# Expert stage of a one-layer diffusion transformer: its pools in another place, each tile waiting for the bytes it takes over

## The chip, the cores and the metric

The kernel runs on one core of a Trainium2 chip. The metric is the device time of one execution in microseconds (us). A core has five engines with instruction streams of their own: TensorE (PE, matmuls), VectorE (DVE), ScalarE (ACT), GpSimd (POOL) and SyncE (SP, which here only issues transfers). Sixteen DMA engines move data between HBM and the on-chip memory SBUF; matmuls write to the accumulator memory PSUM. Each engine runs its instructions in order, and an instruction that waits holds up everything behind it on that engine.

## The reference

It is one layer on 1024 tokens of width 1024, with a context of 256 tokens: modulation from a condition, windowed attention with a short convolution beside it, a merge, and then a layer of product-key experts, with a norm at the end. The part that matters here is the last one:

```python
def chunk(t):                                    # t: 128 tokens of h
    T = t.shape[0]
    qh = (t @ w_q).reshape(T, 8, 2, 128)         # 8 heads, two halves of a query
    s = jnp.einsum('thpd,hpnd->thpn', qh, sub_keys)
    s_top, i_top = lax.top_k(s, 16)              # 16 of 128 keys for each half
    cand = s_top[:, :, 0, :, None] + s_top[:, :, 1, None, :]
    cand_idx = i_top[:, :, 0, :, None] * 128 + i_top[:, :, 1, None, :]
    best, pos = lax.top_k(cand.reshape(T, 8, 256), 16)
    idx = jnp.take_along_axis(cand_idx.reshape(T, 8, 256), pos, axis=-1)
    g = jax.nn.softmax(best, axis=-1)
    ue, ve = u_tab[idx], v_tab[idx]              # 16384 experts, rows of 1024
    act = jax.nn.gelu(jnp.einsum('thkd,td->thk', ue, t), approximate=False)
    return jnp.einsum('thk,thkd->td', g * act, ve)
```

## The kernel before

**Two halves.** The tokens are worked on in two halves of 512. For each half the kernel computes queries and scores (`bank` in PSUM, split by ACT into a 16-bit high part `qqh` and by DVE into a low part `qql`), and finds the top 16 keys on DVE (`sl`, `sv`, `si`). The scores use weights `whl` that SP loads one after another (line 170) into four buffers of the pool `wts`. For half 0 the gates are then scattered into a dense table in HBM, `gd` (written by POOL from `ge`, line 1008), while the scores of half 1 are still being worked out.

**The expert stage** begins at 1096 us of the trace and runs to the end. It treats most experts densely: 128 slots of 128 experts. For a slot SP loads 128 rows of `v` (line 1131), two slots ahead the rows of `u` (`u_t`, line 1114), for every 16 slots two gate tiles `gt` (line 1091), and PE makes `ups` = u times the tokens. ACT applies GELU (`gel`), DVE multiplies `gel` by `gt`, ACT writes the 16-bit high part `wdh` and DVE the low part `wdl`; `v` is split in the same way into `vh` (ACT) and `vl` (DVE); and PE sums the products of these parts into PSUM tiles `res` and `vps`. The slots run first with all 512 tokens of half 0, then with 384 of half 1.

**Slots 0 to 2** have their GELU values prepared earlier (`UPRE` = 3): they lie in HBM as `ged` and only have to be loaded (line 1168). The `u` rows of slots 3 to 5 are split into `whl` buffers before the stage (`u_first`, line 1453): their 72 matmuls, `ups<-h,whl`, are the first PE work of the stage.

**Beside the slots** run the gates of half 1: DVE finds the best candidates (`cand`, `best`, `pos`), turns them into indices (`eq`, `fi`, `fig`, `ci`), and POOL gathers 512 tiles of `u` rows and 128 of `v` rows by these indices (`row`, line 916), which DVE multiplies with the tokens (`row<-row,hn`) and adds up.

**Pools.** SBUF is cut into pools that open and close as a stack, from a left and a right end. Before the expert stage the left end holds, counted in KB of each partition behind the constants, `wts` (24 KB, with the `whl` buffers), `half1` (32 KB), and on the bytes of `half0` the pool `gate0`, in which the gates of half 0 are worked on. All of them are closed before the stage, and `psF` and others in PSUM too. The stage opens `acc` (14 KB: sums `part` and buffers `wdh`) and on top of it `dense0`, with everything else: loads, `gel`, `gt`, splits. So the first tiles of `dense0` lie on bytes of `wts`. By default the first use of any tile in a new pool waits until everything that used the released pools below it has ended. `gate1` is opened on the right for the gates of half 1.

**Order.** The framework's scheduler decides the order of the instructions of each engine up to slot 8 of the stage (`PIN_FROM`); from there on the code pins it. Nearly all instructions of PE, DVE and ACT are recorded by a helper (class `Meter`), so they all have line 72; they are told apart by their tiles.

Of the kernel before, what the change touches and what calls it, by code (L numbers as in the profile page):

```python
# [11 lines left out]
F16 = mybir.dt.float16  # L12
# [6 lines left out]
PSUM = bass.MemoryType.PSUM  # L19

D = 1024
# [10 lines left out]
NDENSE = 512  # L32
NMIX = 384
# [9 lines left out]
SUB = 4  # L43
# [71 lines left out]
def drain(gen):  # L115
    while True:
        try:
            next(gen)
        except StopIteration as e:
            return e.value  # L120


class K:
# [9 lines left out]
        self.waiting = []  # L133
        self.turned = None

    def pool(self, name, side=None, space=None, bufs=1):
        kw = {}
        if side is not None:
            kw["side"] = side
        if space is not None:  # L140
            kw["space"] = space
        g = self.tc.tile_pool(name=name, bufs=bufs, **kw)
        p = g.__enter__()
        return g, p
# [870 lines left out]
    def open_gate(self, name, side, ge_bufs):  # L1015
        nc, a = self.nc, self.a
        self.ge_bufs = ge_bufs
        g, self.pg = self.pool(name, side=side)
        p = self.pg
        io32 = p.tile([128, 128], F32, name="io32", tag="dot", bufs=1)  # L1020
        nc.sync.dma_start(io32, a["iota"])
        io16 = p.tile([128, 128], F16, name="iotas")
        nc.vector.tensor_copy(io16, io32)
        self.iota = io16.rearrange("p (a b) -> p a b", b=REP).unsqueeze(1).to_broadcast([128, TB, 128 // REP, REP])
        self.cand = p.tile([128, 8, NCAND], F32, name="cand", tag="cand", bufs=1)
        nc.vector.memset(self.cand[:, :, 16:128], NEG)
        self.iota16 = p.tile([128, 16, 16], F16, name="iota16")
        nc.vector.tensor_copy(self.iota16, io32[:, 0:16].unsqueeze(2).to_broadcast([128, 16, 16]))
        return g
# [104 lines left out]
    def split_v(self, i1, v32, p):  # L1134
        if v32 is None:
            return self.vparts[i1]
        vh = p.tile([128, D], F16, name="vh", tag="vh", bufs=2 * SUB)
        vl = p.tile([128, D], F16, name="vl", tag="vl", bufs=2 * SUB)
        self.nc.scalar.activation(vh, v32, AF.Copy, scale=16.0)
        self.late[0].append((vl, v32, 16.0, vh))  # L1140
        if i1 >= 128 - 2 * SUB:
            self.vparts[i1] = vh, vl
        return vh, vl
# [13 lines left out]
    def slot_dense(self, i1, p, pv, outs):  # L1157
        nc = self.nc
        nb = NDENSE // 32
        hh, hl = self.h2h[0], self.h2l[0]  # L1160
        self.load_u(i1 + 2, p)
        v32 = self.load_v(0, i1, p)
        self.block_gates(0, i1, p)
        wh = self.pac.tile([128, NDENSE], F16, name="wdh", tag="wdh", bufs=2 * SUB)
        wl = p.tile([128, NDENSE], F16, name="wdl", tag="wdl", bufs=2 * SUB)
        ge = p.tile([128, NDENSE], F32, name="gel", tag="gel", bufs=2)
        if i1 < UPRE:
            nc.sync.dma_start(ge, self.ged[i1])
        else:
            uh, ul = self.uparts.pop(i1)  # L1170
            ps = pv.tile([128, 512], F32, name="ups", tag="v", bufs=3)
            for k in range(8):
                self.mm3(ps, uh[:, k, :], ul[:, k, :], hh[:, k, :], hl[:, k, :], k == 0, k == 7)
        self.lows(1)
        self.lows(0)
        if outs:
            yield 0
        if i1 >= UPRE:
            nc.scalar.activation(ge, ps, AF.Gelu, scale=2.0 ** -12)
        self.split_u(i1 + 2, p)  # L1180
        vh, vl = self.split_v(i1, v32, p)
        ends = []
        for k, out in enumerate(outs):
            ends.append(out())
            if k == 0:
                yield 0
        for end in ends:
            end()
        gev = ge.rearrange("p (b t) -> p b t", t=16)
        for q in range(2):  # L1190
            qs = slice(nb * q, nb * q + nb)
            nc.vector.tensor_mul(gev[:, qs, :], gev[:, qs, :], self.gts[q][:, :, i1 % GR, :])
        nc.scalar.activation(wh, ge, AF.Copy, scale=256.0)
        self.late[0].insert(0, (wl, ge, 256.0, wh))
        yield 0
        return vh, vl, wh, wl

    def slot_mix(self, i1, p, outs):
        nc = self.nc
        nb = NMIX // 32  # L1200
        v32 = self.load_v(1, i1, p)
        self.block_gates(1, i1, p)
        self.lows(0)
        vh, vl = self.split_v(i1, v32, p)
        wh = self.pac.tile([128, NMIX], F16, name="wdh", tag="wdh", bufs=2 * SUB)
        wl = p.tile([128, NMIX], F16, name="wdl", tag="wdl", bufs=2 * SUB)
        parts = [w.rearrange("p (b t) -> p b t", t=16) for w in (wh, wl)]
        for q in range(2):
            qs = slice(nb * q, nb * q + nb)
            g = self.gts[q][:, :, i1 % GR, :]  # L1210
            nc.scalar.activation(parts[0][:, qs, :], g, AF.Copy, scale=256.0)
            self.late[0].insert(q, (parts[1][:, qs, :], g, 256.0, parts[0][:, qs, :]))
        yield 1
        self.lows(0)
        for out in outs:
            out()()
            yield 1
        return vh, vl, wh, wl
# [188 lines left out]
    def run(self):  # L1407
        nc, a = self.nc, self.a
        self.setup()
        self.nsq = 4  # L1410
        self.g_two, self.two = self.pool("psA", space=PSUM)
        self.g_pa, self.pa = self.pool("ps0", space=PSUM)
        self.nbank = 6
        g_pw, self.pw = self.pool("wts", side="left")
        halves = [None, None]
        self.hT, self.cT, self.aT = [None, None], [None, None], [None, None]
        for hf in (1, 0):
            g, p = self.pool(f"half{hf}", side="left")
            halves[hf] = g
            self.hT[hf] = tuple(p.tile([128, 8, HALF], F16, name=f"hT{hf}{i}") for i in range(2))  # L1420
            self.cT[hf] = tuple(p.tile([128, 4, HALF], F16, name=f"cT{hf}{i}") for i in range(2))
            self.aT[hf] = tuple(p.tile([128, 4, HALF], F16, name=f"aT{hf}{i}") for i in range(2))
        self.stage0()
        g_q, self.pq = self.pool("qkv", side="left")
        self.stage1()
        g_s2, self.ps2 = self.pool("s2", side="right")
        self.sv[0] = self.ps2.tile([128, 4, 2, 8, 16], F32, name="sv0")
        self.si[0] = self.ps2.tile([128, 4, 2, 8, 16], U32, name="si0")
        self.nrstd = 1
        self.nsq = 2  # L1430
        st = self.stage2(0)
        self.weave([(self.until(st, "merged"), 24), (self.attends(4, 8), 36)])
        self.close(g_q)
        self.close(self.g_pa)
        self.close(self.g_two)
        self.g_pa, self.pa = self.pool("psQ", space=PSUM)
        self.nbank = 8
        drain(self.until(st, "summed"))
        st1 = self.stage2(1)
        for _ in range(8):  # L1440
            next(st)
        for _ in range(AHEAD):
            next(st1)
        drain(st)
        self.close(self.g_pa)
        g_pf, self.pf = self.pool("psF", space=PSUM)
        self.ftag = ("f", 2)
        self.nbank = 6
        g_pa, self.pa = self.pool("psB", space=PSUM)
        self.close(halves[0])  # L1450
        g_g = self.open_gate("gate0", "left", 2)
        self.run_side(st1, self.gates(0), GATES_B)
        self.u_first = {i: self.weight(None, a["u_t"][i]) for i in range(UPRE, UPRE + 3)}
        self.close(g_g)
        self.close(self.g_x1)
        self.close(g_s2)
        self.close(halves[1])
        self.close(g_pw)
        self.close(g_pa)
        self.close(g_pf)  # L1460
        g_pv, pv = self.pool("psV", space=PSUM)
        self.pf, self.ftag = pv, ("v", 3)
        self.bank = self.fbank
        g_ac, self.pac = self.pool("acc", side="left")
        self.part = self.pac.tile([128, 8 - NRES, HALF], F32, name="part")
        gd, pd = self.pool("dense0", side="left")
        g_g = self.open_gate("gate1", "right", 1)
        self.experts(pd, pv)
        self.close(gd)
        self.close(g_ac)  # L1470
        self.close(g_g)
        self.close(g_pv)
        self.close(self.g_pc)
# [63 lines left out]
```

## Time and profile before

| | |
|---|---|
| time, median of 3 runs | 3055.07 us (3054.99 to 3056.49) |
| time of the profiled execution | 3051.96 us |
| its span, from the first to the last instruction | 3050.2 us |
| PE busy | 2901.6 us, 95% |
| DVE busy | 2648.9 us, 87% |
| ACT busy | 1177.5 us, 39% |
| POOL busy | 1051.9 us, 34% |
| bytes moved | 795.74 MB, 261 GB/s on average |

All later times are positions in this span or lengths inside it. The 1.76 us between the span and the execution's time lie around it. A timeline row gives start, length, engine, line, operation, the tile written and the tiles read, how many were joined (x2), and in brackets the idle time of the engine just before and what ended it. Rows that follow each other closely overlap by some 0.1 us, since an engine takes the next instruction before the last one is through. PEclk is the clock that TensorE was granted, as a share of full speed.

### The profile page before, as it was taken

The page shows a single profiled execution, that of the slowest core. Times are in us where ns is not written, and L with a number is a line of the kernel's source. Part 1 is how long each engine was busy: PE and PEld are TensorE (multiplying, and loading weights), DVE is VectorE, ACT ScalarE, POOL GpSimd, SP SyncE. Part 2 cuts the span into 40 slices and gives each one's busy share as a digit, 9 for nine tenths or more (in the row PEclk, how much of TensorE's full clock was granted, in tenths as well). Part 3 has the DMA queues.
Part 4 walks back from the last instruction along what each step waited for, and adds up shares of the span by engine and source line. Part 5 has one row for each costly group of instructions (what it writes and reads, how often), then busy time and mean ns, then how long its engine had stood idle before and what let it go on. Part 6 is the DMA issues. An engine that isn't in the chain of part 4 may idle for free.

```text
span 3050.2 us, 49089 instructions
## 1 busy us (share of the span) xinstructions
PE 2901.6 (95%) x18685; PEld 1528.4 (50%) x18685; DVE 2648.9 (87%) x5438; ACT 1177.5 (39%) x1878; POOL 1051.9 (34%) x812
## 2 busy tenths in 40 slices
PE   6899999998989978999999999999999989999998
PEld 2455555444444533444444444444444446676775
DVE  7788666599999979999899998999989979888887
ACT  4844466333434323232333332333333333443342
POOL 2100011201211003544444444545444435455553
PEclk9999999999999988999999999999999999999999
DMA  6333434663445547998899998899989988999995
GB/s 223 97 111 93 129 125 122 215 211 132 179 180 190 187 149 258 317 340 301 306 318 342 356 338 297 310 332 335 336 325 343 322 298 305 371 372 355 351 368 193
DMA packets 327197, 795.74 MB, mean 261 GB/s; under 512 B 22960, under 2 KB 147248, under 8 KB 319792
## 3 DMA queue, kind: packets, MB, share of 16 engines
q1 hardware_dynamic: 219536, 372.08, 36.7%
q0 software_dynamic: 103968, 395.36, 35.3%
q10 hardware_dynamic: 3456, 25.17, 2.0%
q8 instruction: 146, 2.39, 0.3%
q14 instruction: 91, 0.75, 0.1%
HBM read 696.31 MB, written 96.21 MB: 260 GB/s over the span
## 4 chain that ended last, share of the span: by engine, by line
PE 58%; DVE 25%; issue 8%; DMA 3%; POOL 3%; ACT 2%; SPq 0%; DVEq 0%; POOLq 0%; ACTq 0%
PE res L72 23%; PE ups L72 13%; PE bank L72 12%; PE vps L72 5%; PE sc L72 4%; DVE row L72 3%; POOL row L916 3%; DVE e L72 2%; DMA row<-u,ci 2%; DVE si L72 2%; DVE eq L72 2%; DVE sv L72 1%; PE fbank L72 1%; DVE vl L72 1%; DVE ah L72 1%
## 5 line engine op out<-in xcount | busy, mean ns | idle before, releaser
L916 POOL DMA_INDIRECT row<-u,ci x512 | 669.7, 1308 | 909.1 <-DVE row L72 647.5
L72 DVE SCALAR_TENSOR_TENSOR row<-row,hn 128x1024 f32<-128x1024 f32 x512 | 614.9, 1223 | 80.8 <-DMA row<-u,ci 62.8
L72 PEld LDWEIGHTS <-vh 128*128 128x128 f16 x5120 | 470.0, 98 | 358.2 <-issue 25.4
L72 PE MATMUL res<-wdl,vh 128*128 128x128 f16 (+2 forms) x2176 | 628.6, 306 | 14.3 <-DVE wdl L72 14.1
L72 PE MATMUL res<-wdh,vh 128*128 128x128 f16 (+2 forms) x2176 | 625.5, 306 | 12.8 <-ACT wdh L72 12.8
L72 PE MATMUL res<-wdh,vl 128*128 128x128 f16 (+2 forms) x2176 | 625.0, 306 | 5.0 <-DVE vl L72 5.0
L72 PE MATMUL ups<-h,uh 128*128 128x512 f16 x1952 | 582.2, 380 | 0.0
L72 PEld LDWEIGHTS <-whl 128*128 128x128 f16 x3288 | 316.5, 99 | 369.4 <-issue 47.3
L72 PE MATMUL bank<-hT,whl 128*128 128x512 f16 x1584 | 378.4, 388 | 14.3 <-ACT hT L72 5.7
L72 ACT ACTIVATE vh<-v 128x1024 f16<-128x1024 f32 x248 | 260.5, 1050 | 304.7 <-DMA v<-v 127.5
L72 PE MATMUL ups<-h,ul 128*128 128x512 f16 x976 | 370.9, 380 | 5.7 <-DVE ul L72 5.6
L72 PEld LDWEIGHTS <-vl 128*128 128x128 f16 x2560 | 251.0, 98 | 197.4 <-DVE vl L72 24.3
L72 DVE SCALAR_TENSOR_TENSOR vl<-v,vh 128x1024 f16<-128x1024 f32 x248 | 301.9, 1218 | 11.8 <-ACT vh L72 11.8
L72 PEld LDWEIGHTS <-uh 128*128 128x128 f16 x1952 | 191.0, 98 | 228.7 <-issue 2.5
L916 POOL DMA_INDIRECT row<-v,ci x128 | 212.6, 1661 | 178.4 <-DVE wdl L72 92.4
L72 ACT ACTIVATE gel<-ups 128x512 f32<-128x512 f32 x125 | 74.6, 597 | 391.8 <-PE ups L72 376.3
L72 ACT ACTIVATE wdh<-gel 128x512 f16<-128x512 f32 x128 | 80.6, 631 | 369.2 <-DVE gel L72 341.3
L72 ACT ACTIVATE ge<-fbank 128x512 f32<-128x512 f32 x224 | 121.7, 594 | 219.8 <-PE fbank L72 187.4
L72 DVE SCALAR_TENSOR_TENSOR racc<-row,fig,racc 128x1024 f32<-128x1024 f32 x127 | 162.6, 1281 | 9.5 <-DMA row<-v,ci 8.5
L72 DVE TENSOR_TENSOR e<-iotas,ii 128x1024 f16<-128x1024 f16 x224 | 153.0, 707 | 6.1 <-ACT ii L72 4.8
L72 PEld LDWEIGHTS <-ul 128*128 128x128 f16 x976 | 95.7, 98 | 123.0 <-DVE ul L72 7.7
L72 PE MATMUL vps<-wdh,vh 128*128 128x512 f16 x384 | 145.5, 379 | 5.2 <-ACT ge L72 3.6
(222 smaller groups left out, 4223.7 us busy)
## 6 DMA issues: line engine op xcount, KB each, us to landing
v<-v SPq DMA_DIRECT2D x248, 512.0 KB
u<-u_t SPq DMA_DIRECT2D x122, 512.0 KB
gd<-ge POOLq DMA_DIRECT2D x32, 1024.0 KB
gt<-gd SPq DMA_DIRECT2D x32, 1024.0 KB
wm<-w_mod SPq DMA_DIRECT2D x48, 512.0 KB
gd<-ge ACTq DMA_DIRECT2D x24, 1024.0 KB
gt<-gd SPq DMA_DIRECT2D x32, 768.0 KB
w<-w_in SPq DMA_DIRECT2D x34, 512.0 KB
```

The costliest lines, as they stand in the source:

```text
L72: r = f(*args, **kw)
L916: self.nc.gpsimd.indirect_dma_start(out=r, out_offset=None, in_=tab, in_offset=bass.IndirectOffsetOnAxis(ap=ci[:, s:s + 1], axis=0))
```

## The change

Three things change. A new pool `parts` is opened first on the left: it takes `vh`, `vl` and `wdl` (40 KB) out of `dense0`. Behind it comes `acc`, and then `dense0`, which so starts 54 KB behind the constants in place of 14 KB, about where `gate0` was. And five pools (`psV`, `parts`, `acc`, `dense0`, `gate1`) are opened with `reuse_waits="tile"`: a tile in them waits for the users of those earlier tiles that lay on its own bytes, and for no others.

```diff
-    def pool(self, name, side=None, space=None, bufs=1):
-        kw = {}
+    def pool(self, name, side=None, space=None, bufs=1, **kw):
...
-        g, self.pg = self.pool(name, side=side)
+        g, self.pg = self.pool(name, side=side, reuse_waits="tile")
...
-        vh = p.tile([128, D], F16, name="vh", tag="vh", bufs=2 * SUB)
-        vl = p.tile([128, D], F16, name="vl", tag="vl", bufs=2 * SUB)
+        vh = self.ppt.tile([128, D], F16, name="vh", tag="vh", bufs=2 * SUB)
+        vl = self.ppt.tile([128, D], F16, name="vl", tag="vl", bufs=2 * SUB)
...
-        wl = p.tile([128, NDENSE], F16, name="wdl", tag="wdl", bufs=2 * SUB)
+        wl = self.ppt.tile([128, NDENSE], F16, name="wdl", tag="wdl", bufs=2 * SUB)
...
-        g_pv, pv = self.pool("psV", space=PSUM)
+        g_pv, pv = self.pool("psV", space=PSUM, reuse_waits="tile")
...
-        g_ac, self.pac = self.pool("acc", side="left")
+        g_pt, self.ppt = self.pool("parts", side="left", reuse_waits="tile")
+        g_ac, self.pac = self.pool("acc", side="left", reuse_waits="tile")
         self.part = self.pac.tile([128, 8 - NRES, HALF], F32, name="part")
-        gd, pd = self.pool("dense0", side="left")
+        gd, pd = self.pool("dense0", side="left", reuse_waits="tile")
```

The scheduler sees other waits and so puts the instructions around the start of the stage in another order. From about the sixth slot on (about 1150 to 1160 us) DVE, PE and ACT have the same order in both kernels, and POOL has it throughout.

**SP, the end of the weight loads of half 1.** Before, all weights (`whl<-ws_...`) come first, and the expert stage's first load of `v` waits for a list of semaphores with PE's at its end (DMAHW are semaphores of SP's transfers, DMASW of POOL's):

```order
L170 DMA whl<-ws_wq_7208 128x2048 [waits DMAHW7_49,DMAHW2_49,PE_49]
L170 DMA whl<-ws_wq_7279 128x2048 [waits DMAHW3_49,DMAHW0_49,PE_49]
L173 DMA w_11963<-u_t 128x1024 [waits DVE_49]
L1021 DMA io_11987<-iota 128x128 [waits DVE_49,DMAHW5_49,Activation_49,Pool_49]
L925 DMA hn_12441<-h2d 128x1024
L1131 DMA v_11995<-v 128x1024 [waits DMASW6_49,DMASW5_49,DMASW7_49,DMASW4_49,DMAHW1_49,DMASW3_49,DMAHW2_49,DMASW2_49,DMAHW3_49,DMASW1_49,DMAHW4_49,DMASW0_49,PE_49]
L1091 DMA gt<-gd_92 128x16x128 x2
L1168 DMA gel<-ged_10238 128x512
L1131 DMA v_12022<-v 128x1024
L1168 DMA gel<-ged_10272 128x512
```

In the change the same loads stand among the weights, behind a wait for DVE and for the stores of `gd`:

```order
L811 DMA h2d<-hn 128x4x128 [waits DMAHW1_49,Activation_49]
L1130 DMA v_11998<-v 128x1024 [waits DVE_49]
L1090 DMA gt<-gd_92 128x16x128 [waits DMASW4_49,DMASW5_49,DMASW3_49,DMASW6_49,DMASW2_49,DMASW7_49,DMASW1_49,DMAHW3_49,DMASW0_49,DVE_49]
L811 DMA h2d<-hn 128x4x128 [waits DMAHW4_49,Activation_49]
L169 DMA whl<-ws_sk_6811 128x2048 [waits DMAHW5_49,PE_49]
L1090 DMA gt<-gd_92 128x16x128 [waits DMASW7_49,DMASW5_49,DMAHW6_49,DMASW3_49,DMASW1_49]
L169 DMA whl<-ws_wq_6853 128x2048 [waits DMAHW7_49,PE_49]
L811 DMA h2d<-hn 128x4x128 [waits DMAHW0_49,Activation_49]
L1167 DMA gel<-ged_10238 128x512 [waits DMAHW1_49]
L1130 DMA v_12025<-v 128x1024 [waits DMAHW2_49]
L1167 DMA gel<-ged_10272 128x512 [waits DMAHW3_49]
```

The first of them moves from behind the last weight to the place behind the store of `h2d` that SP issues at 1025.76 us. In all, four `v` tiles, four `gt` tiles and two `gel` tiles go ahead of the last weights.

**DVE, the end of the scores of half 1.** The last scores are `si`. Before, `vl`, the first `gel` products and then the candidates follow:

```order
L72 MEMSET cand 128x8x112
L72 TENSOR_SCALAR g2r<-g2s 128x8
L72 CAST iotas<-io_11987 128x128
L72 CAST iota_11993<-io_11987 128x256
L72 SCALAR_TENSOR_TENSOR vl<-v_11995,vh 128x1024
L72 TENSOR_TENSOR gel<-gel,gt 128x256 x2
L72 CAST fi<-si_86 128x256
L72 TENSOR_TENSOR cand<-sv_85 128x8x16
```

In the change the candidates, the first `best` and `pos` come ahead of `wdl` and `vl`:

```order
L72 TENSOR_SCALAR g2r<-g2s 128x8
L72 CAST iotas<-io_11990 128x128
L72 CAST iota_11996<-io_11990 128x256
L72 MAX best<-cand 128x8 x4
L72 MAX_INDEX pos<-best,cand 128x8 x4
L72 SCALAR_TENSOR_TENSOR wdl<-gel,wdh 128x512 x2
L72 SCALAR_TENSOR_TENSOR vl<-v_11998,vh 128x1024
L72 SCALAR_TENSOR_TENSOR vl<-v_12025,vh 128x1024
L72 TENSOR_TENSOR gel<-gel,gt 128x256 x2
```

`fi` and the `cand` sums stand right behind the memset now, ahead of this piece. The first four `gel` products have left it: they stand among the scores, one about 1066 us and three about 1070 us by the times that their neighbours have in the trace of before. The first `wdl` waits for the last of the 72 `ups<-h,whl` matmuls, since its bytes lay under a `whl` buffer.

**ACT, in the scores of half 1.** `wdh` of the first two slots is made from those products, so it stands there too, ahead of a `qqh` and an `sl`:

```order
 L72 ACTIVATE qqh<-bank 128x512
 L72 ACTIVATE sl<-bank 128x512
-L72 ACTIVATE qqh<-bank 128x512
+L72 ACTIVATE wdh<-gel 128x512
+L72 ACTIVATE qqh<-bank 128x512
+L72 ACTIVATE wdh<-gel 128x512
 L72 ACTIVATE sl<-bank 128x512
```

The two `wdh` have moved ahead from their places behind the last `sl`. The first three `vh` follow right behind the last `sl`, ahead of any `wdh`. On PE the order is as before, but the 72 matmuls no longer wait for ACT's last `sl`.

## Rows read from the trace of the kernel before

**Rows 1.** The page: busy time of each engine with its instructions.

```profile
PE 2901.6 (95%) x18685; PEld 1528.4 (50%) x18685; DVE 2648.9 (87%) x5438; ACT 1177.5 (39%) x1878; POOL 1051.9 (34%) x812
```

**Rows 2.** Windows: start:end, then for each engine busy us; PEclk, DMA share, GB/s.

```profile
1055.00:1104.75 49.75, 46.36 (x274) 23.61 (x273) 49.75 (x299) 11.46 (x18) 0.00 (x0) 0.93 0.16 54
1104.75:1124.60 19.85, 9.22 (x43) 4.12 (x42) 2.48 (x6) 1.06 (x1) 0.00 (x0) 0.82 0.61 194
1124.60:1168.20 43.60, 35.77 (x149) 14.80 (x149) 43.60 (x151) 20.58 (x26) 0.00 (x0) 0.89 0.55 185
1200.00:2450.00 1250.00, 1233.54 (x6151) 576.13 (x6149) 1160.08 (x2023) 413.39 (x557) 595.06 (x449) 1.00 0.92 326
```

**Rows 3.** Timeline of PE: the scores' end, the stage's start, the waits behind.

```profile
1056.12 0.38 PE L72 MATMUL bank<-h2h,whl 128*128 128x512 f16 x1
...
1094.33 0.29 PE L72 MATMUL bank<-whl,qql 128*128 128x128 f16 x1 [2.64 <-DVE qql L72]
...
1096.31 17.66 PE L72 MATMUL ups<-h,whl 128*128 128x512 f16 x72 [0.73 <-ACT sl L72]
1126.08 1.01 PE L72 MATMUL res<-wdh,vh 128*128 128x512 f16 x2 [12.11 <-ACT wdh L72]
...
1167.28 0.61 PE L72 MATMUL ups<-h,ul 128*128 128x512 f16 x1 [4.89 <-DVE ul L72]
```

**Rows 4.** Chain of waits that ended last, from the stage's start: start, us, what.

```profile
1114.85 3.02 SPq L1091
1117.91 6.60 DMA gel<-ged
...
1127.20 0.67 DVE gel L72 x2
```

**Rows 5.** Timeline of SP: transfers issued around the stage's start.

```profile
1025.76 0.37 SPq L812 DMA_DIRECT2D h2d<-hn  x1
...
1048.86 24.65 SPq L170 DMA_DIRECT2D whl<-ws_wq  x6
...
1114.00 0.33 SPq L1131 DMA_DIRECT2D v<-v  x1
1114.38 3.49 SPq L1091 DMA_DIRECT2D gt<-gd  x2
...
1150.47 0.33 SPq L1131 DMA_DIRECT2D v<-v  x1
```

**Rows 6.** Timeline of DVE: from the stage's first v split to the first dots.

```profile
1118.99 1.23 DVE L72 SCALAR_TENSOR_TENSOR vl<-v,vh 128x1024 f16<-128x1024 f32 x1 [11.77 <-ACT vh L72]
1124.60 0.76 DVE L72 TENSOR_TENSOR gel<-gel,gt 128x256 f32<-128x256 f32 x2 [4.39 <-DMA gel<-ged]
...
1126.52 0.69 DVE L72 SCALAR_TENSOR_TENSOR wdl<-gel,wdh 128x512 f16<-128x512 f32 x1
1127.12 0.76 DVE L72 TENSOR_TENSOR gel<-gel,gt 128x256 f32<-128x256 f32 x2
...
1129.68 0.67 DVE L72 SCALAR_TENSOR_TENSOR wdl<-gel,wdh 128x512 f16<-128x512 f32 x1
...
1167.88 0.28 DVE L72 SCALAR_TENSOR_TENSOR ci<-fig 128x128 int32<-128x128 f32 x1
...
1174.90 1.23 DVE L72 SCALAR_TENSOR_TENSOR row<-row,hn 128x1024 f32<-128x1024 f32 x1 [4.33 <-DMA row<-u,ci]
```

**Rows 7.** Timeline of ACT: the first wdh, and a vh that waits for its load.

```profile
1125.40 0.63 ACT L72 ACTIVATE wdh<-gel 128x512 f16<-128x512 f32 x1 [6.44 <-DVE gel L72]
...
1154.00 1.06 ACT L72 ACTIVATE vh<-v 128x1024 f16<-128x1024 f32 x1 [0.45 <-DMA v<-v]
```

**Rows 8.** Timeline of POOL: the last store of the gate table of half 0.

```profile
1025.54 0.53 POOL L1008 DMA_DIRECT2D gd<-ge  x1 [7.04 <-ACT ge L72]
```

**Rows 9.** Windows, columns as in rows 2: a stretch of the scores, and one behind ci.

```profile
1042.00:1074.00 32.00, 30.29 (x192) 15.64 (x191) 32.00 (x201) 6.66 (x13) 0.00 (x0) 1.00 0.33 108
1176.60:1182.90 6.30, 0.08 (x2) 0.00 (x0) 4.29 (x7) 0.50 (x1) 3.22 (x3) 0.68 1.04 382
```

More of the change, by code (lines that the diff above doesn't have):

```diff
@@ L1205, in slot_mix @@
         wh = self.pac.tile([128, NMIX], F16, name="wdh", tag="wdh", bufs=2 * SUB)
-        wl = p.tile([128, NMIX], F16, name="wdl", tag="wdl", bufs=2 * SUB)
+        wl = self.ppt.tile([128, NMIX], F16, name="wdl", tag="wdl", bufs=2 * SUB)
         parts = [w.rearrange("p (b t) -> p b t", t=16) for w in (wh, wl)]
@@ L1470, in run @@
         self.close(g_ac)
+        self.close(g_pt)
         self.close(g_g)
```

## Prediction

> **What bounds the kernel now.** I read the profile's page first: PE is busy 95% of the span and DVE 87% [rows 1], so the question is where either of them stands still. The windows by stage answer it [rows 2]. From 1200 to 2450 us PE works 1233.54 of 1250 us and there is little to gain. During the scores of half 1 (1055 to 1104.75) DVE is busy for all of 49.75 us. Between that and the steady part there is a hole: from 1104.75 to 1124.60 DVE works 2.48 of 19.85 us, so it stands still for 17.37, and PE works 9.22. Right behind it DVE is at 43.60 of 43.60 us again, and PE at 35.77.
>
> Next, the timeline of PE shows what it does in the hole [rows 3]: the 72 matmuls of `u_first` run from 1096.31 for 17.66 us, to 1113.97, and then PE is idle for 12.11 us until the first `res` matmul, at 1126.08. The chain of waits says what filled those 12 us [rows 4]: not work, but the issue of loads for 3.02 us and the landing of a `gel` load for 6.60 us. The timeline of SP completes it [rows 5]: the first `v` load of the expert stage is issued at 1114.00, as the 72 matmuls end, and `gt` at 1114.38. So the loads of the first slots, which need nothing from those matmuls, wait for them only because their pool lies on released bytes.
>
> What matters behind the hole is DVE: from 1124.60 it works without a break to `ci` at 1167.88 [rows 6], the index list for POOL's gathers. PE waits there for DVE, not the other way: 4.89 us for `ul` at 1167.28 [rows 3] and some 6.2 us in the window 1176.60:1182.90, where it works 0.08 of 6.30 us [rows 9]. So I follow DVE through the change; PE's hole ends with it.
>
> **The change part by part.**
>
> *The loads move.* By the order, four `v`, four `gt` and two `gel` loads go among the weight loads of half 1, the first behind the `h2d` store at 1025.76 [rows 5], and the `gt` loads behind the last store of `gd`, issued at 1025.54 [rows 8]. That takes the 3.02 and 6.60 us of the chain [rows 4] off the path: ten loads are in SBUF well before 1096. Bytes: 4 x 512 KB, 4 x 1024 KB and 2 x 256 KB are 6.8 MB. At the pace of 1104.75:1124.60, 194 GB/s at a share of 0.61 [rows 2], full engines move 318 GB/s, so these are 21.4 us of all sixteen. From 1042 to 1074 their share is 0.33 [rows 9], which leaves 0.67 x 32 = 21.4 us, and there is room before and behind. I cost them at nothing; what it costs without that room is the rival below that ends slower.
>
> *Four `gel` products move into the scores.* DVE has no gap there [rows 2], so they push the scores back by their length: a pair takes 0.67 us in the chain [rows 4], two pairs 1.34.
>
> *Two `wdh` on ACT move among the scores*, each ahead of a part that the scores need, and each waits for its `gel` product. Behind them in ACT's order stand a `qqh` and an `sl`, for which DVE and PE wait. One `wdh` is 0.63 us [rows 7]. No row shows such a crossing. From below it is nothing, if ACT has the time; from above it is the two `wdh` and as much again for the ways to and from DVE, 2.5. I take 1.1, nearer the lower middle, since ACT works only 11.46 of 49.75 us in that stretch [rows 2]. Scores late: 1.34 + 1.1 = 2.44 us.
>
> *PE.* The last score matmuls start at 1094.33 and took until the idle 0.73 ahead of 1096.31, that is 1.25 us [rows 3]. The 72 matmuls no longer wait for ACT's `sl` and follow directly: 1094.33 + 2.44 + 1.25 = 1098.02, and with 17.66 they end at 1115.68.
>
> *DVE around their end.* DVE is through with the scores at 1104.75 + 2.44 = 1107.19. Then it has work it did later before: memset, `g2r` and the casts, 2.48 - 1.23 (`vl`) = 1.25 [rows 2, 6]; `fi` and `cand`, the time between the `gel` pair and `wdl`, 1126.52 - 1124.60 - 0.68 = 1.24; and `best` and `pos`, 1129.68 - 1127.12 - 0.67 = 1.89 [rows 6]. In sum 4.38, so at 1111.57 it comes to the first `wdl`. That tile lies where a `whl` buffer was, and waits for the last of the 72 matmuls. Here is what is late next: DVE stands for 4.1 us, until about 1115.75, and queued behind this wait are `vl`, `gel` and the rest of the candidates.
>
> *From there to `ci`.* Before, 1167.88 - 1124.60 = 43.28 us [rows 6]. Of these 1.24 and 1.89 are done already, and so are two `gel` pairs, 0.68 and 0.67: 4.48 less. The first `vl`, 1.23 alone and 1.2 in a row, comes in. 43.28 - 4.48 + 1.2 = 40.0 us. One new wait: the third `gel` load still takes over a buffer that the first `wdl` reads, so it is issued some 0.7 us behind 1115.75, and DVE wants it after two `wdl` and two `vl`, 3.5 us behind 1115.75. A `v` load of twice its size took from 1150.47 to 1154.00 [rows 5, 7], 3.5 us, and a `gel` load in the crowded hole 6.60 [rows 4]. So the wait is between 0 and 3.8; I take 0.7, by the nearer row of 3.5 (0.7 + 3.5 - 3.5). Then `ci` is at 1115.75 + 40.0 + 0.7 = 1156.45, which is 11.4 us earlier.
>
> PE keeps up: its work between 1126.08 and the idle before 1167.28 was 1167.28 - 4.89 - 1126.08 = 36.3 us; it now starts at 1115.7 and `ul` is due at 1155.85, so 3.8 us of idle are left. As a control on DVE: 17.37 us of idle go, and 4.1, 0.7 and 1.1 come, which gives 11.5.
>
> Opening the gap from the other side gives nearly the same. The Trainium skill, page "Perfetto Trace Analysis", section "Optimization Strategy", says to take the most contended engine, find the gaps on it and let what blocks it start sooner. By that rule it is PE, and its 12.11 us less the 1.7 by which the 72 matmuls end later would give 10.4 us, against 11.4 by DVE; the trace has PE waiting for DVE behind the gap, so I stay with DVE.
>
> *`psV`, `acc`, `gate1` with waits by tile.* `io` and `hn` no longer wait for the end of the scores, and what DVE waited for them lies inside the 17.37 us. I cost them at nothing; without that cover it is no more than what is left of those 17.37 besides the waits of 11.77 for `vh` and 4.39 for `gel` [rows 6], 1.2 us.
>
> *Behind `ci`* the order of every engine is as before, and no transfer stands still in absolute time, so everything moves forward by the same amount: **3051.96 - 11.4 = 3040.6** for an execution like the profiled one. The median of the runs is 3055.07, 3.1 us above that one, so I predict 3055.07 - 11.4 = **3043.7 us**.
>
> **Rivals.**
>
> *The waits behind `ci` shrink too.* DVE waits 4.33 us for the first gathered rows [rows 6], and PE 6.2 us [rows 9], at a DMA share of 1.04. With 6.8 MB of loads done earlier the DMA engines could be emptier there, and those 6.2 us could go as well: 3037.5. Against it: the `u` and `v` loads that fill the engines there are tied to buffers, and move forward together with `ci`.
>
> *Part is given back.* Every crossing and load at its upper bound (1.4 more for ACT, 3.1 more for `gel`) leaves 6.9 us: about 3048.
>
> *All of it is given back*, or the loads come no earlier. If DVE's first `wdl` is not all that waits for the 72 matmuls, the hole stays: 3055, within 0.2% of before (6.1 us, about what a measurement of this kernel can tell from no change). The order speaks against it, since the loads stand there ahead of the weights and wait for DVE and stores alone; that the change does nothing at all is hardly possible.
>
> *Slower: the early loads starve the scores.* SP is one queue in order, and the weights of half 1 stand behind the moved loads. The tightest of them is issued at 1048.86 and PE uses it at 1056.12 [rows 3, 5], 7.3 us later. If the 21.4 us of moved bytes all pass ahead of weights and `whl` loads are held up one after another, PE and with it DVE are late by up to 21.4 us: 3043.7 + 21.4 = 3065. It decides from 11.4 us of starving on, and is measurable as slower from 17.5. The share of 0.33 [rows 9] speaks against it.
>
> The Trainium skill, page "DMA: Bandwidth & Descriptors", section "Issuing engines are not separate DMA queues", states that transfers run on the same 16 DMA engines and interleave whichever engine started them, which speaks for this rival. No row of before shows such a mix of weights and expert loads.
>
> **Numbers.** Forecast 0.56: 3043.7, of its own between 3040.5 (ACT and `gel` free, and 1.4 for the spread) and 3047. Waits behind `ci` shrink too: 0.16. Part given back: 0.08. All given back: 0.13. Slower: 0.07. So faster 0.80, same 0.13, slower 0.07. The range has to reach to the second and third case and a little into the fourth: 3036.5 to 3052.5 leaves out the 0.07, some 0.10 of the fourth and little of the second.
>
> **What would show it.** Right: `v` issued near 1026, the first `vh` on ACT right behind the last `sl` (near 1099), the first `res` at about 1115.7 without a 12 us hole ahead of it, DVE idle only from about 1111.6 to 1115.7, `ci` near 1156.5, and PE's waits for `ul` and `wdl` still there. Wrong: PE or DVE waiting for `whl` between 1030 and 1096; a wait on `gel` above 1.5 us; or a `ci` that comes earlier while the waits behind it grow by the same.

## The result, and the profile after

Measured together, five runs each: the change 3041.0 us in the median (3036.6 to 3042.48), the kernel before 3056.49 us (3054.99 to 3061.58). The ratio is 0.9949, with a 95% interval of 0.9938 to 0.9959: 15.5 us or 0.51% faster, by the interval 12.5 to 19. Measured again on another occasion, beside three of the experiments, the change gave 0.9962 (0.9948 to 0.9975), 11.3 us by the medians. The forecast was 11.4 us, the forecast median 3043.7, its range 3036.5 to 3052.5: the time lies within it.

The profiled execution spans 3035.0 us, 15.2 less than that of before. Busy time has hardly changed, so nothing got cheaper (page of the change, busy time of each engine; before: [rows 1]):

```profile
PE 2897.1 (95%) x18685; PEld 1526.2 (50%) x18685; DVE 2649.4 (87%) x5438; ACT 1175.6 (39%) x1878; POOL 1052.4 (35%) x812
```

The loads. SP's timeline of the change has the first `v` load at 1025.15 and `gt` right behind it, where before they stood at 1114.00 and 1114.38 [rows 5]. The third `gel` load is still late, at 1114.44, since its buffer is read until then:

```profile
1025.15 0.50 SPq L1130 DMA_DIRECT2D v<-v  x1
1026.01 0.78 SPq L1090 DMA_DIRECT2D gt<-gd  x1
...
1042.01 0.51 SPq L1167 DMA_DIRECT2D gel<-ged  x1
...
1114.44 0.33 SPq L1167 DMA_DIRECT2D gel<-ged  x1
```

ACT's timeline shows the two `wdh` among the scores (1070.00 and 1071.01), and three `vh` right behind the last `sl`, at 1097.47, where before the first `vh` waited until 1117.90 for its load:

```profile
1070.00 0.63 ACT L72 ACTIVATE wdh<-gel 128x512 f16<-128x512 f32 x1 [8.21 <-DVE gel L72]
...
1071.01 0.62 ACT L72 ACTIVATE wdh<-gel 128x512 f16<-128x512 f32 x1
...
1097.47 2.94 ACT L72 ACTIVATE vh<-v 128x1024 f16<-128x1024 f32 x3
```

PE's timeline, beside [rows 3]: the 72 matmuls follow the scores without the wait for `sl`, and the first `res` follows them without a gap. The hole of 12.11 us is gone. What is left are the waits for `ul` (4.16) and, behind `ci`, for `wdl` (7.52):

```profile
1095.64 0.29 PE L72 MATMUL bank<-whl,qql 128*128 128x128 f16 x1 [4.99 <-DVE qql L72]
...
1096.68 17.00 PE L72 MATMUL ups<-h,whl 128*128 128x512 f16 x72
1113.52 0.38 PE L72 MATMUL res<-wdh,vh 128*128 128x512 f16 x1
...
1153.07 0.39 PE L72 MATMUL ups<-h,ul 128*128 128x512 f16 x1 [4.16 <-DVE ul L72]
...
1169.36 0.58 PE L72 MATMUL res<-wdl,vh 128*128 128x512 f16 x1 [7.52 <-DVE wdl L72]
```

DVE's timeline, beside [rows 6]: the four `gel` products among the scores, then the new wait ahead of the first `wdl`, 3.23 us for the 72 matmuls; the third slot's products start at 1117.20 without waiting for their load, and `ci` comes at 1153.67, 14.2 us sooner than before:

```profile
1064.54 0.43 DVE L72 TENSOR_TENSOR gel<-gel,gt 128x256 f32<-128x256 f32 x1
...
1069.55 0.75 DVE L72 TENSOR_TENSOR gel<-gel,gt 128x256 f32<-128x256 f32 x2
...
1113.72 1.29 DVE L72 SCALAR_TENSOR_TENSOR wdl<-gel,wdh 128x512 f16<-128x512 f32 x2 [3.23 <-PE ups L72]
...
1117.20 0.75 DVE L72 TENSOR_TENSOR gel<-gel,gt 128x256 f32<-128x256 f32 x2
...
1153.67 0.29 DVE L72 SCALAR_TENSOR_TENSOR ci<-fig 128x128 int32<-128x128 f32 x1
...
1161.19 1.23 DVE L72 SCALAR_TENSOR_TENSOR row<-row,hn 128x1024 f32<-128x1024 f32 x1 [4.84 <-issue]
```

**Where the 15.2 us come from.** Runs of one program differ already ahead of the change: the last store of `gd` (POOL) was issued at 1025.54 before and 1024.51 after, and in the ten profiles here it lies between 1024.51 and 1032.98, though the order of work up to there is the same. So I count from that store. From it to `ci` it took 142.34 us before and 129.16 after: **13.18 us** are the change's. 1.03 us came from ahead of the store, and 0.99 from behind `ci` (1882.32 and 1881.33 us to the end). The stretch behind `ci` lies between 1878.0 and 1883.4 us in nine of the ten profiles (the tenth, dots_later, has another order there), so a difference of one there says nothing.

This table is the ruler for all that follows. Each number is the start of a row in a timeline, or a difference of two: the last `gd<-ge` on POOL; PE's last wait for `qql`, that is the end of the scores on PE; the 72 matmuls `ups<-h,whl`; `ci` on DVE; and the span's end.

| kernel | store | store to last `qql` wait | 72 matmuls, us | store to `ci` | `ci` to the end |
|---|---|---|---|---|---|
| before | 1025.54 | 68.79 | 17.66 | 142.34 | 1882.32 |
| the change | 1024.51 | 71.13 | 17.00 | 129.16 | 1881.33 |
| change_again | 1025.95 | 71.14 | 17.00 | 129.17 | 1882.38 |
| layout_only | 1025.88 | 71.13 | 18.25 | 131.20 | 1882.62 |
| waits_only | 1026.91 | 68.77 | 16.52 | 131.11 | 1879.48 |
| more_loads | 1026.22 | 71.13 | 17.03 | 129.19 | 1877.99 |
| dots_later | 1028.97 | 71.13 | 18.02 | 130.18 | 1884.65 |
| vl_first | 1026.28 | 71.14 | 17.04 | 128.06 | 1882.56 |
| products_later | 1025.97 | 68.79 | 18.15 | 128.04 | 1879.09 |
| both_moves | 1032.98 | 68.79 | 17.39 | 125.59 | 1883.43 |

The way from the store to `ci` has to be read beside the length of the 72 matmuls. They are the same work in every kernel, but they last 16.52 to 18.25 us (the last section has more on it). In the change, change_again, more_loads and dots_later DVE does the same work up to `ci`, and store to `ci` less the length of the matmuls is 112.16 or 112.17 us in all four. So dots_later's 130.18 is 1.02 us later than the change for that length alone.

### The profile page after: what moved, and what is told of

It is laid out like the page before. It is cut to its first block, busy times and chain, and to the rows that moved or that the text cites. A ratio compares the mean times of both kernels' runs of the same rounds, so it can differ in the third digit from the quotient of the medians.

```text
span 3035.0 us, 49079 instructions
## 1 busy us (share of the span) xinstructions
PE 2897.1 (95%) x18685; PEld 1526.2 (50%) x18685; DVE 2649.4 (87%) x5438; ACT 1175.6 (39%) x1878; POOL 1052.4 (35%) x812
## 4 chain that ended last, share of the span: by engine, by line
PE 36%; issue 10%; DVE 8%; POOL 5%; DMA 2%; ACT 0%; POOLq 0%; DVEq 0%; ACTq 0%
PE res L72 21%; PE ups L72 10%; POOL row L915 5%; PE vps L72 4%; DVE row L72 3%; DMA row<-u,ci 2%; DVE vl L72 1%; PE fbank L72 1%; DVE ul L72 1%; DVE wdl L72 1%; DVE acc L72 0%; DVE eq L72 0%; ACT ge L72 0%; DVE gel L72 0%; DVE part L72 0%
```

## The experiments

The theory to be tried is the prediction's: ten loads that start early are worth 11 to 13 us on DVE's way to `ci`, and the weights do not suffer. The rivals ask which edit does it, whether weights are held up, and whether DVE really sets the end there.

**1. The layout alone.** The new pool and the new places stay; every `reuse_waits="tile"` goes:

```diff
-        g_pt, self.ppt = self.pool("parts", side="left", reuse_waits="tile")
-        g_ac, self.pac = self.pool("acc", side="left", reuse_waits="tile")
+        g_pt, self.ppt = self.pool("parts", side="left")
+        g_ac, self.pac = self.pool("acc", side="left")
...
-        gd, pd = self.pool("dense0", side="left", reuse_waits="tile")
+        gd, pd = self.pool("dense0", side="left")
```

> The pool parts and the new places of acc and dense0, but every pool with the default waits. Theory (the early loads are what counts, whatever lets them start): in this kernel's order the ten loads stand among the weights just as in the change, so the gain is nearly whole. What is lost: the 72 matmuls wait for ACT's last sl again (0.7 us), and vh, vl and wdl all wait for the end of the 72 matmuls, so that the first res matmul comes one vh (1.1 us) behind them; DVE has two wdl to do meanwhile. ci near 1154.5, 0.5 to 1 us behind the change; ratio to before 0.995 to 0.996. Rival (the waits by tile bring it): the hole of 10 us or more is back, ratio 0.999 to 1.000.

Measured: 3042.24 us against 3052.98, ratio 0.9961 (0.9948 to 0.9974), and `ci` 131.20 us behind the store, 2.0 later than in the change. The loads start early all the same (SP's timeline):

```profile
1030.52 0.33 SPq L1130 DMA_DIRECT2D v<-v  x1
...
1043.38 0.50 SPq L1167 DMA_DIRECT2D gel<-ged  x1
```

The 2.0 us are more than the 0.5 to 1 that were expected. The price of the coarser waits stands where it was expected, on PE ahead of the 72 matmuls (0.73) and of the first `res` (1.15 for `vh`):

```profile
1098.84 18.25 PE L72 MATMUL ups<-h,whl 128*128 128x512 f16 x72 [0.73 <-ACT sl L72]
1118.24 0.39 PE L72 MATMUL res<-wdh,vh 128*128 128x512 f16 x1 [1.15 <-ACT vh L72]
```

Of the 2.0 us, 0.79 is the longer way from the last `qql` wait to the 72 matmuls (1.83 against 1.04) and 1.25 their length (18.25 against 17.00), which need not be the edit's: dots_later has 18.02 with the waits of the change. Nothing of the 2.0 is left for the 1.15 us ahead of `res`, so they cost DVE nothing. So the layout alone brings nearly all. It also corrects a sentence of the section on the kernel before: a tile in a new pool does not wait for all users of all released pools, else `v` could not start at 1030.52 here. What held it back before is, as these two kernels show, what lay at its pool's place: `dense0` at 54 KB no longer lies on `wts`.

**2. The waits alone.** No pool `parts`, `vh`, `vl` and `wdl` in `dense0` as before, which starts behind `acc`; the four pools that are left wait by tile:

```diff
-        g_pt, self.ppt = self.pool("parts", side="left", reuse_waits="tile")
...
-        vh = self.ppt.tile([128, D], F16, name="vh", tag="vh", bufs=2 * SUB)
+        vh = p.tile([128, D], F16, name="vh", tag="vh", bufs=2 * SUB)
```

> The five pools wait tile by tile, but nothing is moved: no pool parts, dense0 right behind acc. The order of the engines is that of before; the first v load waits only for the first 24 of the 72 matmuls, whose weights lie on its bytes. Theory (the early loads are what counts): v is issued near 1102.3 in place of 1114.0, and all that follows moves up by 11.7 us: the first gel product near 1113, no long PE hole; ratio to before about 0.996, the same as the layout alone. Rival (the place of the pools is needed): the loads still start too late to fill the hole, gain under 4 us, ratio 0.9987 to 1.000.

(The expectation says five pools; without `parts` there are four.) Measured: 3042.41 us, ratio 0.9965 (0.9952 to 0.9978), `ci` 131.11 us behind the store. The rival falls: with the old layout too the gain is nearly whole, but by another way. SP issues `v` at 1102.91, when the first third of the 72 matmuls is through, and DVE still waits 5.68 us for the landing of `gel` where it waited 4.39 us at 1124.60 [rows 6] (SP's timeline, then PE's, then DVE's):

```profile
1102.91 0.33 SPq L1130 DMA_DIRECT2D v<-v  x1
```

```profile
1096.72 16.52 PE L72 MATMUL ups<-h,whl 128*128 128x512 f16 x72
1116.27 1.01 PE L72 MATMUL res<-wdh,vh 128*128 128x512 f16 x2 [3.03 <-ACT wdh L72]
```

```profile
1107.84 1.23 DVE L72 SCALAR_TENSOR_TENSOR vl<-v,vh 128x1024 f16<-128x1024 f32 x1 [0.44 <-ACT vh L72]
1114.74 0.76 DVE L72 TENSOR_TENSOR gel<-gel,gt 128x256 f32<-128x256 f32 x2 [5.68 <-DMA gel<-ged]
```

The scores are not late here (68.77 us), since no product stands among them; a PE gap of 3.03 us is left. So each of the two edits alone takes away some 11 us (11.14 and 11.23 from the store to `ci`). Both together bring 2 us more than either, but of the 2.0 us over the layout alone only 0.8 are clearly due to the waits by tile; the rest is the length of the 72 matmuls. The two gains do not add up, since they remove the same wait.

**3. More loads among the weights.** Eight copies of 1 MB, for nothing, among the last weight loads:

```diff
+        if i1 == 4:
+            more = self.tc.dram_tile([8, 128, 128, 16], F32, name="more")
+            for k in range(8):
+                nc.sync.dma_start(more[k], self.gd[0][31])
```

> The change, with eight copies of 1 MB more (a block of the gate table to another place in HBM, for nothing) issued by SP among the last weight loads, behind the ten early loads: 8.4 MB on top of 6.8 MB. It tries the rival that the early loads starve the scores. Theory (there is room): PE and DVE wait no longer for weights than in the change, ci within 1 us of the change's 1153.7, ratio to before 0.994 to 0.996. Rival (starving): 8.4 MB are 26 us of all sixteen DMA engines; weights or the last u_t load come late, PE waits for whl by several us up to 20, and the ratio is 0.997 to 1.003.

Measured: 3037.0 us, ratio 0.9953 (0.9939 to 0.9966), `ci` 129.19 us behind the store, as in the change (129.16), and the scores at 71.13 as there. The windows show how full the DMA engines are at the weights (columns as in [rows 2]); first the change, where the share is 0.74 in place of 0.33 [rows 9], then this kernel, where it is 0.96:

```profile
1041.00:1073.00 32.00, 30.29 (x192) 15.62 (x191) 31.18 (x189) 7.56 (x15) 0.00 (x0) 1.00 0.74 239
```

```profile
1043.00:1075.00 32.00, 30.29 (x193) 15.53 (x192) 31.18 (x190) 7.57 (x14) 0.00 (x0) 1.00 0.96 335
```

The copies do not stand quite where the expectation has them. Six of the eight (6.3 MB) come ahead of the last weight load, `w<-u_t`; two come behind it, and so does the last of the ten early loads, a `gt` (SP's timeline):

```profile
1057.16 0.58 SPq L1164 DMA_DIRECT2D more<-gd  x1
...
1085.64 0.34 SPq L172 DMA_DIRECT2D w<-u_t  x1
1086.03 1.10 SPq L1164 DMA_DIRECT2D more<-gd  x2
1087.17 0.58 SPq L1090 DMA_DIRECT2D gt<-gd  x1
```

From 1030 to 1100 PE's matmuls waited for `qql` alone, and for no load of weights (waits: total, times, longest):

```profile
PE bank L72 <- DVE qql L72: 8.5, 5, 5.0
```

So the cover holds with nine early loads and six copies ahead of the last weights, 5.8 + 6.3 = 12.1 MB, about 1.8 times what the change moves, and the rival of starving falls. PE never came to a weight that had not landed. The Trainium skill, page "DMA: Bandwidth & Descriptors", section "Issuing engines are not separate DMA queues", has all transfers interleave on the same 16 engines, whichever engine started them. Here SP starts weights, loads and copies alike, so this run shows nothing of the starting engine; it shows these engines shared at 0.96, and that the sharing cost the weights nothing that PE waited for.

**4. The first row products later.** The waits behind `ci` were a rival of the forecast. Here the first three gathers start three turns ahead of their products:

```diff
+        ahead = []
+        if t == 0:
+            for s in range(3):
+                ahead.append(self.row(self.a["u"], ci, s))
+                yield
         for s in range(128):
-            r = self.row(self.a["u"], ci, s)
+            r = ahead.pop(0) if ahead else self.row(self.a["u"], ci, s)
```

> The change, with the first three gathers issued three turns ahead of their dots: DVE's first three row products come behind the next ul, wdl and vl in place of ahead of them, and each later product three turns later. It tries what the waits behind ci are worth, where DVE stands for 7.5 us and PE for 7.5 us ahead of wdl. Theory (these waits are on the path that sets the end): PE's 7.5 us shrink to 1 or 2, the steady part starts 4 to 7 us sooner, ratio to the kernel before 0.993. Rival (they are made up for, or the wait only moves to the next row product, or the three products cost their 3.7 us at the end): as the change, 0.9945 to 0.9955.

Measured: 3043.19 us, ratio 0.9961 (0.9947 to 0.9975): no gain over the change is shown. The windows from `ci` on (25, then 175 us) show what became of the wait; first the change, then this kernel:

```profile
1153.67:1178.67 25.00, 16.92 (x61) 6.57 (x59) 17.52 (x38) 3.75 (x5) 11.71 (x11) 0.73 1.00 352
1178.67:1353.67 175.00, 173.84 (x805) 78.54 (x804) 169.53 (x341) 55.13 (x70) 90.72 (x68) 1.00 0.91 324
```

```profile
1159.15:1184.15 25.00, 25.00 (x107) 10.87 (x105) 19.24 (x41) 6.12 (x8) 13.70 (x10) 0.91 1.01 359
1184.15:1359.15 175.00, 169.40 (x782) 76.07 (x780) 166.92 (x344) 52.81 (x68) 88.32 (x67) 1.00 0.91 323
```

PE does win 8.1 us in the first 25 (25.00 busy against 16.92): that part of the theory is right. In the next 175 it works 4.4 us less than in the change. How far the lead lasts can be read from the starts of DVE's `vl` splits, one for nearly every slot, counted from `ci`, beside the nine other profiles:

| | dots_later | the nine others |
|---|---|---|
| third `vl` behind `ci` | 19.9 | 24.6 to 25.9 |
| 61st | 648.3 | 649.2 to 653.7 |
| last | 1840.8 | 1839.2 to 1844.4 |
| from the last `vl` to the end | 43.87 | 38.73 to 39.07 |

At 650 us this kernel is still ahead of every other; at the last slot it lies within their spread. What is certain is the end, which takes 5 us longer here than anywhere else. There six row additions `racc` stand behind the last `vl`, where the change has three, and the last three wait for their gathers (DVE's timeline of change_again, then of this kernel):

```profile
2998.67 1.22 DVE L72 SCALAR_TENSOR_TENSOR vl<-v,vh 128x1024 f16<-128x1024 f32 x1
2999.80 2.60 DVE L72 SCALAR_TENSOR_TENSOR racc<-row,fig,racc 128x1024 f32<-128x1024 f32 x2
3002.72 1.28 DVE L72 SCALAR_TENSOR_TENSOR racc<-row,fig,racc 128x1024 f32<-128x1024 f32 x1 [0.32 <-DMA row<-v,ci]
```

```profile
2999.93 1.22 DVE L72 SCALAR_TENSOR_TENSOR vl<-v,vh 128x1024 f16<-128x1024 f32 x1
3001.06 3.92 DVE L72 SCALAR_TENSOR_TENSOR racc<-row,fig,racc 128x1024 f32<-128x1024 f32 x3
3005.92 1.28 DVE L72 SCALAR_TENSOR_TENSOR racc<-row,fig,racc 128x1024 f32<-128x1024 f32 x1 [0.93 <-DMA row<-v,ci]
3009.32 1.29 DVE L72 SCALAR_TENSOR_TENSOR racc<-row,fig,racc 128x1024 f32<-128x1024 f32 x1 [2.11 <-DMA row<-v,ci]
3012.07 1.28 DVE L72 SCALAR_TENSOR_TENSOR racc<-row,fig,racc 128x1024 f32<-128x1024 f32 x1 [1.46 <-DMA row<-v,ci]
```

So of the rival the last branch holds: the three turns by which all row work comes later are paid for at the end, with 5 us where 3.7 were expected. What a wait behind `ci` is worth by itself this run does not show, since it takes the wait away and lengthens the end at once; no run here does the first without the second.

**5. to 8. What is left of the new wait, and the price of the products in the scores.** Three kernels were run beside the change itself.

> The change itself once more, on the same chip as the next three, to be compared with them. Theory: from the last store of the gate table (line 1008 before) to the last wait of the scores on PE 71.1 us, and to ci 129.2 us, as in its first profile; ratio to before 0.994 to 0.996.

Measured: 3039.99 us against 3051.24, ratio 0.9962 (0.9948 to 0.9975), 71.14 and 129.17 us: the two stretches repeat to 0.01 us, since here the 72 matmuls too last 17.00 us as in the change, while the time spreads by some us.

`vl_first` allocates `vl` ahead of `wdl`, so that `vl` lies on the `whl` buffers:

```diff
+        if i1 == 0:
+            self.vl0 = self.ppt.tile([128, D], F16, name="vl", tag="vl", bufs=2 * SUB)
         wl = self.ppt.tile([128, NDENSE], F16, name="wdl", tag="wdl", bufs=2 * SUB)
```

> The change, with the places of vl and wdl in the pool parts exchanged: vl takes the bytes of the whl buffers, wdl those of the last loads and of half1. Nothing else is moved. Theory (DVE sets the end here, and stands for 3.2 us until the 72 matmuls are through, because wdl waits for them): the first two wdl, 1.2 us, run in that idle time, and vl waits in their place; ci comes 1.2 us sooner, 128.0 us behind the last store of the gate table in place of 129.2. The time itself moves by less than a measurement tells. Rival (PE or the third gel load sets the end): ci stays at 129.2.

Measured: 3040.19 us, ratio 0.9964 (0.9951 to 0.9977); `ci` at 128.06 us, 1.1 sooner, where 128.0 was expected. The two `wdl` run without a wait, and the wait is now at `vl`. Its row names ACT's `vh`, but what ended then are the 72 matmuls, at 1098.46 + 17.04 = 1115.50 (DVE's timeline):

```profile
1112.16 1.28 DVE L72 SCALAR_TENSOR_TENSOR wdl<-gel,wdh 128x512 f16<-128x512 f32 x2
1115.59 2.36 DVE L72 SCALAR_TENSOR_TENSOR vl<-v,vh 128x1024 f16<-128x1024 f32 x2 [2.15 <-ACT vh L72]
```

So DVE sets the end there, not PE: PE's work was the same.

`products_later` binds the products of slots 0 and 1 behind the last split of `u` weights:

```diff
+            with self.tc.issue_after(self.split3) if i1 < 2 else nullcontext():
                 nc.vector.tensor_mul(gev[:, qs, :], gev[:, qs, :], self.gts[q][:, :, i1 % GR, :])
```

> The change, with the gel products of the first two slots bound to stand behind the split of the last u weights on DVE: in the order they and the two wdh leave the scores and stand behind the last si and the last sl. Theory (of the 2.34 us by which the scores end later, 1.34 are the products and 1.0 is the crossing to ACT, and the products fit into DVE's 3.2 us of idle time): the scores are as long as before (68.8 us from the last store of the gate table to PE's last wait, in place of 71.1), the 72 matmuls end 2.3 us sooner, DVE still stands for about 1.9 us ahead of wdl, and ci comes 2.3 us sooner, 126.8 us behind that store. Rival (the scores are late because the early loads slow the weights): still 71.1 us, ci 129 or later.

Measured: 3039.26 us, ratio 0.9956 (0.9940 to 0.9972). The scores take 68.79 us as before the change: the 2.34 us were the products and their way over ACT, all of it, and nothing of the loads. But `ci` came at 128.04, not 126.8. The missing 1.2 us are the 72 matmuls: 18.15 us in place of 17.00, at a lower granted clock. The windows of 8 us from PE's last `qql` wait on, first of change_again and then of this kernel, have it at 0.77 and 0.62:

```profile
1097.00:1105.00 8.00, 7.91 (x36) 3.94 (x37) 8.00 (x50) 3.43 (x4) 0.00 (x0) 0.77 0.00 1
```

```profile
1094.70:1102.70 8.00, 7.94 (x31) 3.69 (x32) 8.00 (x50) 0.60 (x1) 0.00 (x0) 0.62 0.00 1
```

`both_moves` has both edits.

> Both of the last two together: vl and wdl exchanged, and the products behind the scores. Theory: 1.2 and 2.3 us add up, ci 125.6 us behind the last store of the gate table; 3.5 us sooner than in the change, a ratio to before of 0.993 to 0.9945. Rival (one of them fills the idle time that the other needs): 126.8, as with the products alone.

Measured: `ci` 125.59 us behind the store, 3.58 sooner than in the change, as expected (125.6). That it fits this closely is luck: the matmuls took 17.39 us, 0.39 more than in the change, and started 0.57 us behind PE's last `qql` wait, 0.47 sooner than there. 3035.82 us, ratio 0.9948 (0.9934 to 0.9961), against 0.9962 of the change on the same chip: 4.2 us by the medians. The intervals overlap, so that the time is lower is not shown beyond its spread; that `ci` is earlier is. DVE's wait has shrunk from 3.2 to 0.69 us:

```profile
1119.82 2.36 DVE L72 SCALAR_TENSOR_TENSOR vl<-v,vh 128x1024 f16<-128x1024 f32 x2 [0.69 <-ACT vh L72]
```

It has the lowest median of the four kernels run beside each other here, and is the kernel that I would go on with.

## Why the prediction was right

- **What bounds the kernel.** Right: the hole was DVE's and PE's wait for loads that needed nothing from the 72 matmuls. Each edit that lets them start brings it, alone.
- **Loads cost nothing.** Right: 6.8 MB at a share of 0.74, and in more_loads six copies more at 0.96, without a wait of PE for weights.
- **Scores late by 2.44 us.** Measured 2.34 (71.13 - 68.79). 1.34 is what the four products take in a row; the other 1.0 I put down to the crossing to ACT, for which I had taken 1.1 without a row, so that it came this near is luck. In the change DVE waits in the scores for ACT's `qqh` and `sl`, 0.5 and 0.3 us, where before and in products_later it waits for nothing there; the last 0.2 is in no wait. products_later shows that the sum has no part that comes from the loads.
- **The 72 matmuls.** I put their end at 1115.68, 90.14 us behind the store. Measured 1113.68 - 1024.51 = 89.17. They follow the scores 1.04 us behind the last wait in place of 1.25, took 17.00 us in place of 17.66, and the scores were 0.1 us less late. The 0.66 of their length is chance as far as the runs show: dots_later has 18.02 for the same work.
- **DVE's wait for them.** 4.1 us predicted, 3.23 measured, less because they ended sooner.
- **From there to `ci`.** 40.0 and a wait of 0.7 predicted; 1153.67 - 1113.72 = 39.95 measured. The 40.0 was right to 0.05 us. The 0.7 was mis-sized: the third `gel` load, issued at 1114.44, had landed when DVE came to it at 1117.20, so it took under 2.8 us, less than the 3.5 of the twice larger `v` load that I had used.
- **Sum to `ci`.** 11.4 predicted, 13.18 measured. The 1.75 between them are 0.97 (end of the matmuls), 0.75 (no `gel` wait, and 40.0 against 39.95) and rounding. The other way of counting, by PE's gap, gave 10.4: the first `res` came 11.53 us sooner behind the store (89.01 against 100.54), and PE still waited 4.16 us for DVE's `ul` behind it, so DVE was the engine to count by.
- **Behind `ci`.** The shift carries through to the end of the profile: that stretch differs by 0.99 us, less than the 5.4 by which it varies among the nine profiles of like order. The rival that the waits there shrink is wrong: DVE waited 4.84 for the first row, 4.33 before [rows 6], and PE 7.52 for `wdl`. What shrinking them would have brought stays open, as dots_later pays for it at the end.

The rest of the way from 13.2 to the measured 15.5 is no part of the mechanism: 1.03 us of the profiled difference came ahead of the change, and the second measurement gave 11.3.

One thing the prediction had too narrow, though the number did not need it: it says that the loads wait only because their pool lies on released bytes. waits_only leaves the pool on those bytes and frees the loads by the grain of the waits. The order of the changed kernel does not tell which of the two edits moved them.

## What to carry to other kernels

A load that waits for nothing but bytes is found where the chain of waits shows an issue and a landing behind the end of unrelated work. Either its pool's place or the grain of the pool's waits can free it, so try the cheaper one alone first. Price it by the engine that works without a gap behind the hole (here DVE, product by product), and count moved work twice when it stands in a stretch where that engine has no gap: once for itself (here 1.34 us) and once for its way over another engine (1.0). And with runs that spread by 3 to 5 us, measure an edit of 1 to 3 us between two rows of the trace, here from a store ahead of it to the index list behind it, where four kernels with the same work up to there agreed to 0.01 us once the length of the 72 matmuls was taken off (to 1.02 us with it). And look at the end of the trace too when an edit delays work: there dots_later lost its 5 us.

## What the runs showed of the hardware

The same 72 matmuls took between 16.52 and 18.25 us in these profiles, and their length goes with the granted clock: 0.92 over their 17.00 us in the change, 0.89 over 17.66 before (windows of the change and of before):

```profile
1096.68:1113.68 17.00, 17.00 (x75) 7.50 (x74) 13.67 (x91) 3.43 (x4) 0.00 (x0) 0.92 0.01 1
```

```profile
1096.31:1113.97 17.66, 17.66 (x72) 7.45 (x71) 9.70 (x63) 0.00 (x0) 0.00 (x0) 0.89 0.11 35
```

The loss is in their first microseconds. In windows of 2 us the change and layout_only have the clock at the lower of its two levels first, 0.50 of full speed (1.2 of 2.4 GHz), and then at the higher; how long the lower one lasts differs (the first and second window of the change, then the second of layout_only, where the first has 0.50 too):

```profile
1096.68:1098.68 2.00, 2.00 (x7) 0.76 (x6) 2.00 (x15) 1.71 (x3) 0.00 (x0) 0.50 0.01 4
1098.68:1100.68 2.00, 2.00 (x9) 0.87 (x8) 2.00 (x15) 1.73 (x2) 0.00 (x0) 0.85 0.00 0
```

```profile
1100.84:1102.84 2.00, 2.00 (x6) 0.76 (x5) 2.00 (x14) 0.00 (x0) 0.00 (x0) 0.50 0.00 0
```

In both_moves the matmuls start at the higher level and fall to the lower a little later: 0.67, 0.50 and 0.98 in the first three such windows. The loss does not go with the length of PE's last wait for `qql` ahead of them: after waits of 4.99 us they took 17.00 (change_again) and 18.02 (dots_later), after waits of 2.63 and 2.64 us 16.52 (waits_only) and 18.15 (products_later). What decides it, no run here shows.
